# Second weight of both feed-forward stages as seven block products, with its input kept in DRAM

## The chip, the cores and the metric

One core of a Trainium2 chip. The metric is the time of the device in microseconds for one launch; the time before is the median of three runs. Matmuls work on float32r operands: every float32 operand is split into a high and a low part, and a product is formed from three matmuls (high x high, high x low, low x high), written `mm3` below.

## The reference

One layer of a streaming encoder for 1024 prompt tokens and 64 sample tokens (1088 columns in all), model width 1024, feed-forward width 2816:

```
h = LN1(alpha*x + 0.5*SwiGLU1(x))
z = h @ w_in; o_a = sparse attention; o_b = chunk-band attention
m = (sigmoid(g_a)*(o_a@w_branch_a) + sigmoid(g_b)*(o_b@w_branch_b)) @ w_out
h = LN2(alpha*h + m)
y = LN3(alpha*h + 0.5*SwiGLU2(h))
SwiGLU(x) = (silu(x@wi_left) * (x@wi_right)) @ wo
```

The two SwiGLU stages are what the change touches. Their first weight `wi` is 1024 x 5632, their second weight `wo` 2816 x 1024.

## The kernel before

Everything is kept transposed: features on the 128 partitions, tokens along the free dimension. `add_ffn7` (line 878) lays down one feed-forward stage as a list of steps; it is called once for each stage, with the bags `G1` and `G2` that hold the stage's tiles.

The 2816 inner features are 22 blocks `f` of 128. Blocks 0 and 1 are computed plainly (`plain`, line 1069). From block 2 on, the first weight is multiplied in Strassen-Winograd form (`product`, line 990): the 1024 input features are halved (2 x 4 parts), the 1088 tokens are halved (`HT` = 544 each), and the two weight columns of a block (left and right of the SwiGLU) are the other halves. Seven products P1, P2, P6, P5, P3, P7, P4 take the place of eight. Each is 2 token quarters (`SUB` = 272 columns) by 4 parts by 3 matmuls, 24 matmuls. Their right factors (tiles A11, A12, A22, S1, S2, S3, S4) are made once per stage: the A by splitting the input, the S by sums (`combos`, line 849; S3, in `third`, goes through the tile `G.t[0]`, named c, which `after` also uses for the copy of P1's bank and for the finished h). Their left factors are weight quarters and differences of them, made per block in `prepare` (line 910).

`after` (line 1024) takes the products from PSUM, applies silu and the product of both halves, and `h_parts` (line 1106) splits the finished h into high and low in a ring of two blocks in SBUF. P5 of a block goes on in the bank that ScalarE has just copied, and P6 goes on in P1's bank, so each waits for that copy (`wait(t[...])` in `product`).

The second weight is multiplied for two blocks at a time (`outputs`, line 1130): for each of 8 output parts `d` and 3 token blocks `b` of 384, 384 and 320 columns, 6 matmuls, then one VectorE addition from PSUM into the float32 tile `y`. This step follows P2 of the next even block; for blocks 0 and 1 it stands between P2 and P6 of block 2. Nine pairs go this way; the last four blocks (18 to 21) are multiplied in `last_outputs` (line 1139), part by part together with the layer norm. The last two blocks, 20 and 21, are computed side by side: P1 and P2 of both, then the other five of each.

Weights come from DRAM in quarters of 128 x 512 on the queue of SyncE (SP), into four to six raw buffers; four split buffers hold what TensorE reads. The order of the instructions is made while the program is built: `Plan` keeps a modelled clock of each engine, tasks have dependencies and priorities, and after every three matmuls (`tick`) the tasks whose modelled start has come are written out. Each engine runs its list in order, and a DMA on SP's list waits there for what it needs. For a task that several engines could take, `shared` and `adders` name VectorE and GpSimd; at the start of each stage (`st["solo"]`, until step `SOLO` = 7) VectorE alone takes them.

## Time and profile before

| | us |
|---|---|
| median of 3 runs | 2550.02 (2547.7 to 2554.39) |
| the profiled execution | 2550.51 |
| its span, first to last instruction | 2548.7 |
| granted TensorE clock, mean over the span | 0.988 |

The first feed-forward stage fills the span up to about 754 us, projections and attention the middle, the second stage begins near 1770 us. Names of engines in the profile: PE is TensorE, DVE VectorE, ACT ScalarE, POOL GpSimd, SP SyncE. Every instruction is recorded at line 119, a helper, so they are told apart by tiles: b is a PSUM bank, w_s a split weight, A and S right factors, h the ring, c the three tiles of `G.t`, y the float32 stream. Matmuls overlap, so a matmul's own duration says little; starts of following groups do.

### The profile page before, as it was taken

How to read it: one execution, taken by the hardware profiler on the slowest of the kernel's cores; microseconds unless marked ns; L12 is line 12 of the kernel's file. 1: busy time of each engine (PE TensorE's matmuls, PEld its weight loads, DVE VectorE, ACT ScalarE, POOL GpSimd, SP SyncE). 2: the span in 40 equal slices, each digit the busy share in tenths (PEclk: the TensorE clock that was granted, in tenths of full speed). 3: DMA queues.
4: the chain of work that ended last, by engine and by line, in shares of the span. 5: the costliest groups of instructions: out<-in, count | busy, mean ns of one | idle time of the engine just before them, and what ended most of it. 6: DMA issues, size and time to landing. Idle time of an engine off the chain costs nothing.

```text
span 2548.7 us, 44883 instructions
## 1 busy us (share of the span) xinstructions
PE 2482.5 (97%) x16906; PEld 2430.8 (95%) x16906; DVE 1794.8 (70%) x4447; ACT 1193.0 (47%) x2561; POOL 387.5 (15%) x515
## 2 busy tenths in 40 slices
PE   9999999999999999999999999999999999999996
PEld 9999999999998999999998999998999999999996
DVE  7666666666675889988676766748866666666667
ACT  5322222223344698677867776515532333222224
POOL 0000000000043322222243432304000000000004
PEclk9999999999998999999999999999999999999997
DMA  5122222111122322223221121643212121111112
GB/s 167 57 69 75 68 67 68 55 59 59 59 73 94 117 75 80 92 78 90 67 80 51 56 64 45 211 131 114 62 59 59 59 59 55 55 54 59 54 51 75
DMA packets 121866, 192.74 MB, mean 76 GB/s; under 512 B 14048, under 2 KB 74832, under 8 KB 121616
## 3 DMA queue, kind: packets, MB, share of 16 engines
q1 hardware_dynamic: 101536, 164.84, 21.2%
q10 hardware_dynamic: 19552, 22.81, 2.9%
q8 instruction: 133, 2.18, 0.4%
q0 software_dynamic: 560, 2.21, 0.2%
q14 instruction: 85, 0.70, 0.1%
HBM read 154.01 MB, written 36.07 MB: 75 GB/s over the span
## 4 chain that ended last, share of the span: by engine, by line
PE 79%; DVE 10%; ACT 6%; issue 2%; POOL 1%; DMA 1%; ACTq 0%; SPq 0%; DVEq 0%; POOLq 0%
PE b L119 79%; ACT w L119 2%; DVE w L119 1%; DVE y L119 1%; DVE w_s L119 1%; ACT scores L119 1%; DVE pt L119 1%; DVE scores L119 1%; DVE c L119 1%; ACT pt L119 1%; DVE k L119 0%; POOL lns L119 0%; DVE sc L119 0%; POOL w_s L119 0%; DVE mk L119 0%
## 5 line engine op out<-in xcount | busy, mean ns | idle before, releaser
L119 PE MATMUL b<-x,w_s 128*128 128x384 f32 (+1 forms) x3528 | 639.4, 332 | 5.1 <-ACT x L119 2.3
L119 PEld LDWEIGHTS b<-x,w_s 128*128 128x128 f32 x3528 | 586.9, 189 | 12.8 <-ACT x L119 2.9
L119 PE MATMUL b<-S,w_s 128*128 128x272 f32 x4032 | 514.3, 288 | 0.0
L119 PEld LDWEIGHTS b<-S,w_s 128*128 128x128 f32 x4032 | 508.6, 188 | 1.0 <-issue 0.6
L119 PE MATMUL b<-A,w_s 128*128 128x272 f32 (+2 forms) x3600 | 477.8, 292 | 3.0 <-ACT c L119 1.3
L119 ACT ACTIVATE w_s<-wr 128x512 fp32r<-128x512 f32 (+1 forms) x318 | 212.7, 670 | 571.4 <-PE b L119 395.1
L119 PEld LDWEIGHTS b<-A,w_s 128*128 128x128 f32 x3600 | 465.6, 190 | 7.5 <-ACT c L119 1.5
L119 PE MATMUL b<-h,w_s 128*128 128x384 f32 (+1 forms) x2736 | 463.8, 328 | 2.8 <-DVE y L119 2.8
L119 PEld LDWEIGHTS b<-h,w_s 128*128 128x128 f32 x2736 | 455.0, 188 | 5.1 <-DVE y L119 3.4
L119 DVE TENSOR_TENSOR w_s<-wr,w_s 128x512 fp32r<-128x512 f32 (+1 forms) x297 | 220.3, 742 | 166.0 <-ACT w_s L119 159.0
L119 DVE TENSOR_TENSOR y<-y,b 128x384 f32<-128x384 f32 (+1 forms) x480 | 251.0, 529 | 119.6 <-PE b L119 117.7
L119 POOL TENSOR_TENSOR w_s<-wr,w_s 128x256 fp32r<-128x256 f32 x196 | 151.8, 800 | 395.6 <-ACT w_s L119 177.7
L119 POOL TENSOR_TENSOR h<-c,h 128x272 fp32r<-128x272 f32 x20 | 15.5, 777 | 1240.5 <-DVE h L119 1239.1
L119 DVE TENSOR_TENSOR c<-c,b 128x272 f32<-128x272 f32 x240 | 103.7, 434 | 74.2 <-PE b L119 74.0
L119 ACT ACTIVATE c<-b 128x272 f32<-128x272 f32 (+1 forms) x262 | 102.0, 391 | 99.5 <-PE b L119 95.7
L119 DVE TENSOR_TENSOR pt<-b,pt 128x512 fp32r<-128x512 f32 (+4 forms) x184 | 96.3, 545 | 28.6 <-ACT pt L119 27.1
L119 ACT ACTIVATE c<-c 128x272 f32<-128x272 f32 x160 | 69.0, 432 | 93.3 <-DVE c L119 91.4
L119 PE MATMUL b<-pt,v 128*128 128x256 f32 (+3 forms) x672 | 103.6, 280 | 4.6 <-DVE pt L119 2.6
L119 PEld LDWEIGHTS b<-pt,v 128*128 128x128 f32 (+1 forms) x672 | 93.8, 188 | 13.5 <-DVE pt L119 5.1
L119 PE MATMUL b<-m,w_s 128*128 128x384 f32 (+1 forms) x576 | 101.5, 337 | 4.0 <-DVE w_s L119 3.8
L119 ACT ACTIVATE w<-w,mx 128x640 f32<-128x640 f32 (+5 forms) x144 | 100.5, 698 | 8.9 <-DVE mx L119 5.8
L119 PEld LDWEIGHTS b<-m,w_s 128*128 128x128 f32 x576 | 98.5, 194 | 5.7 <-DVE w_s L119 4.7
(262 smaller groups left out, 2963.8 us busy)
## 6 DMA issues: line engine op xcount, KB each, us to landing
wr<-in_wi_dram SPq DMA_DIRECT2D x166, 256.0 KB, 2.6
wr<-in_wz_dram SPq DMA_DIRECT2D x35, 512.0 KB, 3.6
wr<-in_wo_dram SPq DMA_DIRECT2D x47, 256.0 KB, 2.8
more<-in_wi_dram SPq DMA_DIRECT2D x38, 256.0 KB, 2.6
wr<-in_wout_dram SPq DMA_DIRECT2D x16, 512.0 KB, 3.8
q<-in_wi_dram SPq DMA_DIRECT2D x28, 256.0 KB, 2.6
g_d<-z ACTq DMA_DIRECT2D x32, 192.0 KB, 1.9
g<-g_d SPq DMA_DIRECT2D x32, 192.0 KB, 2.9
```

What stands on the lines that cost most here:

```text
L119: r = real(*args, **kw)
```

## The change

Of the 22 blocks, the first 18 (`KEPT_OUT`) are no longer multiplied with the second weight as they come. The finished h of each (float32, not split) is written to a DRAM array `ff_d` (`keep`). When the first weight is done, a second part multiplies them, nine pairs in Strassen-Winograd form: the two blocks of a pair are the halves of the inner dimension, the eight output parts are halved (4 and 4), and the tokens are halved. The seven kinds of products come one kind after the other, nine pairs each, and accumulate over the pairs in the eight PSUM banks; 63 products of 4 parts by 2 token quarters by 3 matmuls of 272 columns. After each kind `take_out` adds the banks to y.

The right factors come from h read back (36 tiles `G.a` of 128 x 544), with sums made in place and split into 5 factor buffers (`left`). The weight differences are made in the first part, at P1 of blocks 4 to 12 (`sums_of_weights`), and kept in DRAM (`tw_d`). The tiles of the second part take the memory of the first part's right factors (`to_second1`, `to_second2`). Blocks 18 and 19 are kept in the ring and multiplied as before: output parts 0 and 1 in `early`, between the two parts, the rest in `last_outputs`. Blocks 2 and 3 are computed side by side, as 20 and 21 are. The stream that prepares the bias tables in the first stage starts at block 4.

```diff
+KEPT_OUT = 18
...
+    ff_d = [dram.tile([KEPT_OUT * P, NT], F32, name=f"ff_d{i}") for i in range(2)]
+    tw_d = [dram.tile([P, 2 * KEPT_OUT * 512], F32, name=f"tw_d{i}") for i in range(2)]
...
-            second = f == NF - 1
+            second = f in SECONDS
...
+            def times(name, x, y, deps, cols, reads=()):
+                def go():
+                    nc.vector.scalar_tensor_tensor(x, x, 0.5, y, op0=OP.mult, op1=OP.mult)
+                    keep(f, x, cols)
+                t[name, s] = plan.task("dve", "f_m", go, deps, 1, None, reads)
...
+        def keep(f, x, cols):
+            if f < KEPT_OUT:
+                nc.sync.dma_start(ff[f * P:(f + 1) * P, cols], x)
+
+        def h_parts(o, x, cols, dep):
+            if o.f < KEPT_OUT:
+                return dep
+            h = o.h
...
-        def outputs(f0):
+        def early():
+
+            f0 = KEPT_OUT
             wait(*(F[f].t[x, s] for f in (f0, f0 + 1) for x in ("h1", "h2") for s in range(2)))
-            for i in OUTS[f0 == 0]:
-                u = get_unit(f"o{i}", f0)
-                for d in (2 * i, 2 * i + 1):
-                    for b in range(3):
-                        out_products([f0, f0 + 1], d, b, u.slot, (d % 2) * 2)
-                done_with(u)
+            wait(*G.sums_made)
+            roles.update(mm=[0, 1, 2, 3])
+            for t in range(4):
+                wait(*users.pop(t, ()))
+            G.to_second()
+            G.loads = [(n, j) for n in ("12", "11") for j in range(PAIRS)] + [(n, j) for j in range(PAIRS) for n in ("21", "22")]
+            load(0)
+            for i in range(len(G.fac)):
+                left(i)
+            u = get_unit("o0", f0)
+            for d in (0, 1):
+                for b in range(3):
+                    out_products([f0, f0 + 1], d, b, u.slot, (d % 2) * 2)
+                touched.update((d, half, s) for half in range(2) for s in range(2))
+            done_with(u)
+
+        def load(i):
+
+            while G.loads and 4 * PAIRS - len(G.loads) < 5 + 1.45 * i:
+                n, j = G.loads.pop(0)
+                back.add((n, j))
+                f, half = 2 * j + int(n[1]) - 1, int(n[0]) - 1
+                nc.sync.dma_start(G.a[n, j], ff[f * P:(f + 1) * P, half * HT:(half + 1) * HT])
+
+        def sums_of_weights(j):
+
+            r = G.stage[j % 2]
+            for i in range(4):
+                nc.sync.dma_start(r[i].rearrange("p (d c) -> p d c", d=4),
+                                  wog[:, i % 2 * 4:i % 2 * 4 + 4, (2 * j + i // 2) * P:(2 * j + i // 2 + 1) * P])
+            last = ()
+            for i, out, x, y in ((0, 0, 1, 0), (1, 1, 3, 1), (2, 3, 3, 0), (3, 2, 2, 3)):
+                def go(e, i=i, out=out, x=x, y=y):
+                    of(e).tensor_tensor(r[out], r[x], r[y], op=OP.subtract)
+                    nc.sync.dma_start(tw[:, (4 * j + i) * 512:(4 * j + i + 1) * 512], r[out])
+                last = [plan.task(shared(512), "w_x", go, last, 6, None, [r[x], r[y]])]
+            G.sums_made += last
+
+        def left(i):
+
+            x, j = SECOND[i // PAIRS], i % PAIRS
+            a11, a12, a21, a22 = (G.a[n, j] for n in ("11", "12", "21", "22"))
+            fac = G.fac[i % len(G.fac)]
+
+            def make(out, x, y, op, deps, reads=()):
+                return plan.task(shared(HT), "x_m", lambda e: of(e).tensor_tensor(out, x, y, op=op), deps, 2, None, reads)
+            y, deps = {"P2": a12, "P1": a11, "P6": a11, "P5": a21, "P3": a12, "P7": a11, "P4": a22}[x], []
+            if x == "P6":
+                t1 = sums_of[1, j] = make(a21, a21, a22, OP.add, [], [a21, a22])
+                deps = [make(a11, a21, a11, OP.subtract, [t1] + made["P1", j])]
+                sums_of[2, j] = deps[0]
+            elif x == "P5":
+                deps = [sums_of[1, j]]
+            elif x == "P3":
+                deps = [make(a12, a12, a11, OP.subtract, [sums_of[2, j]] + made["P2", j])]
+                sums_of[4, j] = deps[0]
+            elif x == "P7":
+                deps = [make(a11, a22, a11, OP.subtract, [sums_of[4, j]] + made["P6", j])]
+
+            def hi(e):
+                if e == "act":
+                    nc.scalar.activation(fac[:, 0], y, AF.Copy)
+                else:
+                    nc.vector.tensor_copy(fac[:, 0], y)
+
+            def lo(e):
+                of(e).tensor_tensor(fac[:, 1], y, fac[:, 0].bitcast(F32), op=OP.subtract)
+            assert {(n, j) for n in NEEDS[x]} <= back
+            t1 = plan.task((("act", 93 + 0.84 * HT), ("dve", WH * (69 + 0.52 * HT))), "x_h", hi, deps, 2, None, [y])
+            made[x, j] = [t1, plan.task(adders(HT), "x_l", lo, [t1], 2)]
+
+        def second(i):
+
+            x, j = SECOND[i // PAIRS], i % PAIRS
+            u = get_unit("x" + x, j)
+            wait(*made[x, j])
+            fac, first, final = G.fac[i % len(G.fac)], x in ("P2", "P1", "P7"), j == PAIRS - 1
+            for d in range(4):
+                c = slice(d * P, (d + 1) * P)
+                for s in range(2):
+                    if j == 0 and first:
+                        banks[d, s] = take_bank(2 * d + s)
+                    elif j == 0:
+                        wait(outs[d, s])
+                    p, v = banks[d, s][:, :SUB], fac[:, :, s * SUB:(s + 1) * SUB]
+                    nc.tensor.matmul(p, u.slot[:, 0, c], v[:, 0], start=first and j == 0, stop=False, skip_group_check=True)
+                    nc.tensor.matmul(p, u.slot[:, 0, c], v[:, 1], start=False, stop=False, skip_group_check=True)
+                    nc.tensor.matmul(p, u.slot[:, 1, c], v[:, 0], start=False, stop=final, skip_group_check=True)
+                    tick()
+                    if final:
+                        take_out(x, d, s, p)
+            done_with(u)
+            load(i + 1)
+            if i + len(G.fac) < len(SECOND) * PAIRS:
+                left(i + len(G.fac))
...
+        def take_out(x, d4, s, p):
+            half, d = {"P2": (0, 0), "P1": (0, 0), "P6": (1, 0), "P5": (1, 4), "P3": (0, 4), "P7": (1, 4), "P4": (1, 0)}[x]
+            d += d4
+            y = G.y[d][:, half * HT + s * SUB:half * HT + (s + 1) * SUB]
+            fresh = (d, half, s) not in touched
+            touched.add((d, half, s))
+            if fresh:
+                wait(*G.read[d])
+
+            def go():
+                if fresh:
+                    nc.vector.scalar_tensor_tensor(y, y, ALPHA, p, op0=OP.mult, op1=OP.add)
+                else:
+                    nc.vector.tensor_tensor(y, y, p, op=OP.add)
+            outs[d4, s] = outs[d, half, s, 0] = plan.task("dve", "f_y", go, (), 1, None, [p])
+            if x in ("P2", "P3", "P4"):
+                users[2 * d4 + s] = [outs[d4, s]]
...
+                    wait(*(outs[d, half, s, 0] for half in range(1 + (b > 0)) for s in range(2)))
+                    skip = 2 * (d < 2)
+                    out_products(fs[skip:], d, b, us[d].slot, skip)
...
-        for f in range(EIGHT, NF - 2):
+        def side_by_side(f):
+            return [(x, (f, f + 1)) for x in ("P1", "P2")] + [(x, (g,)) for g in (f, f + 1) for x in FACTOR if x > "P2"]
+        order += side_by_side(EIGHT)
+        for f in range(EIGHT + 2, NF - 2):
+            if f == EIGHT + 2:
+                order.append(("beside", (f,)))
+            if f == KEPT_OUT:
+                order.append(("ring", (f,)))
             for x in FACTOR:
-                if f == 3 and x == "P1" and gi == 0:
-                    order.append(("beside", (f,)))
                 order.append((x, (f,)))
-                if x == "P2" and f % 2 == 0:
-                    order.append(("out", (f - 2,)))
-        last_two = (NF - 2, NF - 1)
-        order += [(x, last_two) for x in ("P1", "P2")] + [(x, (f,)) for f in last_two for x in FACTOR if x > "P2"]
+                if x == "P1" and f - EIGHT - 2 < PAIRS:
+                    order.append(("sums", (f - EIGHT - 2,)))
+        order += side_by_side(NF - 2)
+        order += [("early", (KEPT_OUT,))] + [("second", (i,)) for i in range(len(SECOND) * PAIRS)]
...
+                elif x == "second":
+                    y, j = SECOND[f // PAIRS], f % PAIRS
+                    block = {"P2": (1, 0), "P1": (0, 0), "P3": (1, 1)}.get(y)
+                    if block:
+                        row, col = block
+                        want.append((("x" + y, j), lambda q: q.rearrange("p (d c) -> p d c", d=4),
+                                     wog[:, 4 * col:4 * col + 4, (2 * j + row) * P:(2 * j + row + 1) * P]))
+                    else:
+                        i = 4 * j + {"P5": 0, "P7": 1, "P6": 2, "P4": 3}[y]
+                        want.append((("x" + y, j), lambda q: q, tw[:, i * 512:(i + 1) * 512]))
+                    unit("x" + y, j)
+                    steps.append(lambda f=f: second(f))
...
+    SECONDS = (EIGHT + 1, NF - 1)
+    SECOND, PAIRS = ("P2", "P1", "P6", "P5", "P3", "P7", "P4"), KEPT_OUT // 2
+    NEEDS = dict(P2=("12",), P1=("11",), P6=("11", "21", "22"), P5=(), P3=(), P7=(), P4=())
...
+        G.a = {(x, j): p.tile([P, HT], F32, name=f"a{x}_{j}") for x in ("12", "11", "21", "22") for j in range(KEPT_OUT // 2)}
+        return [p.tile([P, 2, HT], F32R, name=f"fac{i}") for i in range(n)]
...
+    def to_second1():
+        close("x")
+        G1.fac = second_tiles(G1, pool(open_("x"), "back1", "right"), 5)
...
+    def to_second2():
+        close("s4")
+        close("s")
+        G2.fac = [G2.xc["A12"][:, k] for k in range(4)] + second_tiles(G2, pool(open_("s"), "back2"), 1)
```

## Rows read from the trace of the kernel before

**Rows 1.** Page, part 1: engine, busy us (share of the span), instructions.

```profile
PE 2482.5 (97%) x16906; PEld 2430.8 (95%) x16906; DVE 1794.8 (70%) x4447; ACT 1193.0 (47%) x2561; POOL 387.5 (15%) x515
```

**Rows 2.** Waits of TensorE, 90 to 600, then 1860 to 2510: us, times, longest.

```profile
PE b L119 <- DVE c L119: 0.2, 1, 0.2
...
PE b L119 <- DVE acc L119: 0.5, 1, 0.5
```

**Rows 3.** Timeline, TensorE, one output pair per stage: start us, us, what, [idle before].

```profile
602.39 23.98 PE L119 MATMUL b<-h,w_s 128*128 128x384 f32 x144
626.21 12.13 PE L119 MATMUL b<-S,w_s 128*128 128x272 f32 x96
638.18 9.16 PE L119 MATMUL b<-A,w_s 128*128 128x272 f32 x72
...
2363.05 24.10 PE L119 MATMUL b<-h,w_s 128*128 128x384 f32 x144
2386.99 12.19 PE L119 MATMUL b<-S,w_s 128*128 128x272 f32 x96
...
2399.03 9.18 PE L119 MATMUL b<-A,w_s 128*128 128x272 f32 x72
```

**Rows 4.** Timeline, TensorE, last output products of the first stage.

```profile
716.70 1.20 PE L119 MATMUL b<-h,w_e 128*128 128x384 f32 x6
...
747.83 1.04 PE L119 MATMUL b<-A,w_i 128*128 128x320 f32 x6
```

**Rows 5.** Timeline, TensorE, output product of blocks 0 and 1, both stages.

```profile
63.90 3.12 PE L119 MATMUL b<-h,w_s 128*128 128x384 f32 x18
68.72 21.12 PE L119 MATMUL b<-h,w_s 128*128 128x384 f32 x126 [1.70 <-DVE y L119]
...
1833.39 4.21 PE L119 MATMUL b<-h,w_s 128*128 128x384 f32 x24
1838.68 20.17 PE L119 MATMUL b<-h,w_s 128*128 128x384 f32 x120 [1.08 <-DVE y L119]
```

**Rows 6.** Timeline, VectorE, first and last of the S3 sums, both stages.

```profile
61.98 0.73 DVE L119 TENSOR_TENSOR c<-y 128x544 f32<-128x544 f32 x1
...
71.64 0.72 DVE L119 TENSOR_TENSOR S<-c,S 128x544 fp32r<-128x544 f32 x1
...
1833.17 0.72 DVE L119 TENSOR_TENSOR c<-y 128x544 f32<-128x544 f32 x1
...
1849.37 0.72 DVE L119 TENSOR_TENSOR S<-c,S 128x544 fp32r<-128x544 f32 x1
```

**Rows 7.** Timeline, ScalarE, the copy behind them in the first stage.

```profile
72.39 0.69 ACT L119 ACTIVATE c<-b 128x272 f32<-128x272 f32 x2 [0.90 <-DVE S L119]
```

**Rows 8.** Groups by shape: xcount | busy us, mean ns | idle before.

```profile
L119 DVE TENSOR_TENSOR w_s<-wr,w_s 128x512 fp32r<-128x512 f32 x285 | 203.0, 713 | 165.4 <-ACT w_s L119 158.4 <-DMA g<-g_d 0.4
...
L119 DVE TENSOR_TENSOR c<-c,b 128x272 f32<-128x272 f32 x240 | 103.7, 434 | 74.2 <-PE b L119 74.0
...
L119 DVE TENSOR_TENSOR S<-c,S 128x544 fp32r<-128x544 f32 x32 | 22.8, 721 | 6.4 <-ACT S L119 5.8
L119 ACT ACTIVATE S<-c 128x544 fp32r<-128x544 f32 x32 | 20.6, 656 | 37.3 <-DVE c L119 37.3
```

**Rows 9.** DMA issues: tiles, queue, xcount, KB each, us to landing.

```profile
wr<-in_wo_dram SPq DMA_DIRECT2D x47, 256.0 KB, 2.8
...
o_d<-o SPq DMA_DIRECT2D x32, 128.0 KB, 1.7
```

**Rows 10.** Timeline, TensorE, a wait early in the second stage.

```profile
1788.65 1.28 PE L119 MATMUL b<-ones,lns 128*128 128x1 f32 x6 [2.70 <-DVE lns L119]
```

**Rows 11.** Windows: us, busy of PE PEld DVE ACT POOL, PEclk, DMA share, GB/s.

```profile
1788.20:1794.80 6.60, 6.15 (x28) 6.15 (x29) 2.25 (x6) 2.69 (x5) 0.00 (x0) 0.50 0.16 47
...
662.00:704.00 42.00, 42.00 (x338) 42.00 (x338) 28.95 (x59) 15.14 (x32) 1.55 (x2) 1.00 0.22 66
1593.00:1657.00 64.00, 61.16 (x357) 58.96 (x356) 49.10 (x89) 38.03 (x64) 23.45 (x23) 1.00 0.66 211
```

More of the change, by code (lines that the diff above doesn't have):

```diff
@@ L883, in add_ffn7 @@
         free, src, want, units, by, users = list(G.free), {}, [], [], {}, {}
+        ff, tw = ff_d[gi // 2], tw_d[gi // 2]
+        sums_of, made, outs, banks, touched, back = {}, {}, {}, {}, set(), set()
         at, low, F, ACC, Y = Bag(), {}, {}, {}, {}
@@ L1054, in after @@
             elif kind == "P3":
-                times("m1", c, p, [t["s1", s]], [p])
+                times("m1", c, p, [t["s1", s]], one, [p])
                 users[base + s] = [t["m1", s]]
-                t["h1", s] = h_parts(h, c, one, t["m1", s])
+                t["h1", s] = h_parts(o, c, one, t["m1", s])
                 G.user[0, s] = [t["h1", s]]
@@ L1064, in after @@
                 silu("s2", c21, t["c21", s])
-                times("m2", c21, c22, [t["s2", s], t["c22", s]])
-                t["h2", s] = h_parts(h, c21, two, t["m2", s])
+                times("m2", c21, c22, [t["s2", s], t["c22", s]], two)
+                t["h2", s] = h_parts(o, c21, two, t["m2", s])
                 G.user[1, s], G.user[2, s] = [t["h2", s]], [t["m2", s]]
@@ L1123, in out_products @@
             y = Y[d, b]
-            if fs[0] == 0:
+            if (d, 0, 0) not in touched:
                 wait(*G.read[d])
@@ L1262, in tile_trunk, with stage_tiles, ring_tile, second_tiles @@
     factors(G1, sorted(set(FACTOR.values()) - {"A11"}), x1)
-    G1.ring = rp.tile([P, 2, 2, NT], F32R, name="h")
     G1.t = [rp.tile([P, 2, SUB], F32, name=f"c{i}") for i in range(3)]
-    flip, btab = rp.tile([P, P], F32, name="flip"), rp.tile([P, 2, HEADS], F32, name="btab")
     raw_tiles(G1)
     G1.q += [rp.tile([P, 512], F32, name=f"q{i}") for i in range(2)]
-    G1.free, G1.kept = range(5), 5
+    def stage_tiles(G, name, side):
+        p = pool(open_(name), name, side)
+        G.stage = [[p.tile([P, 512], F32, name=f"st{x}{i}") for i in range(4)] for x in range(2)]
+        return p
+    def ring_tile(G, name, side):
+        close(name)
+        G.ring = pool(open_(name), name, side).tile([P, 2, 2, NT], F32R, name="h")
+    def second_tiles(G, p, n):
+        G.a = {(x, j): p.tile([P, HT], F32, name=f"a{x}_{j}") for x in ("12", "11", "21", "22") for j in range(KEPT_OUT // 2)}
+        return [p.tile([P, 2, HT], F32R, name=f"fac{i}") for i in range(n)]
+    p1 = stage_tiles(G1, "top1", None)
+    flip, btab = p1.tile([P, P], F32, name="flip"), p1.tile([P, 2, HEADS], F32, name="btab")
+    def make_ring1():
+        finish_streams()
+        ring_tile(G1, "top1", None)
+    G1.make_ring = make_ring1
+    def to_second1():
+        close("x")
+        G1.fac = second_tiles(G1, pool(open_("x"), "back1", "right"), 5)
+    G1.to_second = to_second1
+    G1.free, G1.one = range(6), rp.tile([P, 512], F32, name="one")
     def halves_of(w, home):
@@ L1286, in bias_tables @@
     def bias_tables():
-        one = G1.q[G1.kept]
+        one = G1.one
         row = one[:HEADS, :384]
@@ L1326, in bias_tables, with start_bias @@
                 yield
-    def start_bias(after):
-        def go():
-            yield from bias_tables()
-            for _ in range(8):
-                yield
-            roles.update(mm=[4, 5, 6, 7])
-            after()
-        beside(go(), 0.3)
+    def start_bias():
+        beside(bias_tables(), 0.3)
     def load_x(half, row, k):
```

51 lines of the change are left out of this document (28 added, 23 removed).

## The prediction

> **What bounds the kernel now.** I read the busy table of the page first: TensorE works for 2482.5 of 2548.7 us, VectorE for 1794.8 [rows 1]. Busy time alone could hide stalls, so the second view is what TensorE waited for: between 90 and 600 us one wait of 0.2 us, between 1860 and 2510 us one of 0.5 us [rows 2]. In both feed-forward stages, then, the time is the number of matmuls by their spacing. What the change takes from that sum arrives in full, and what counts against it is only time in which TensorE has to wait.
>
> **What it removes and adds on TensorE.** The second weight's product of one pair of blocks is 144 matmuls of 384 and 320 columns. In the first stage one such pair starts at 602.39 and what follows starts at 626.21: 23.82 us. In the second stage 2363.05 to 2386.99: 23.94 us [rows 3]. The new form has per pair seven products of 24 matmuls of 272 columns, 168 in all. The trace has that shape in the first weight's products: 96 from 626.21 to 638.18, 124.7 ns each, and 96 from 2386.99 to 2399.03, 125.4 ns each [rows 3]. So a pair costs 20.95 and 21.07 us instead: 2.87 us less nine times, and again 2.87 us nine times, together 51.7 us. The 36 matmuls for blocks 18 and 19 on output parts 0 and 1 come earlier, and their six evictions are one addition more per tile; the count is the same.
>
> Does the spacing of 272 columns hold in the new loop, which changes its accumulator every 3 matmuls instead of every 12? The output products change theirs after 6 (pairs) or 12 (last four blocks), and six of 384 show 1.20 us, six of 320 show 1.04 us: 0.16 us for 6 x 64 columns, 0.42 ns a column, what 2.4 GHz gives [rows 4]. I take 124.7 and 125.4 ns as they stand; 5 ns a matmul more would cost 2 x 1512 x 5 ns = 15 us.
>
> On the other side stands the Trainium skill, "TensorE: Matmul & The Clock Gate", section "Back-to-back issue gap": in a real stream it gives about 81 ns a matmul at 128 columns and about 131 ns at 512. Interpolated (an estimate), a pair would be 16.1 us before and 16.8 us after, and the change would lose about 12 us instead of gaining 52. The trace speaks against it: 512 is not reached and 272 columns already take 124.7 ns.
>
> **Start of the seven products (block 2).** Now the output product of blocks 0 and 1 stands between P2 and P6 of block 2. TensorE waited 1.70 us in it in the first stage and 1.08 us in the second, since the additions into y wait for the factor sums to have read y [rows 5]. These 2.8 us go. But those 24 us are also the cover for VectorE's last factor sums, S3. They begin when the plain blocks are done with the tile c: 61.98 us, and the last of four ends at 72.36; second stage 1833.17 and 1850.09 [rows 6]. P1's copy out of its bank into that same c comes right behind, at 72.39 [rows 7], and P6 of block 2 accumulates in the bank that it copies. Today P6 comes only when the output product ends, near 89.8, so nobody notices. Afterwards only P1 and P2 of block 3 stand between (48 matmuls, 6.0 us): P6 is due 6.0 us after the point where the output product starts today, at 69.9 and 1839.4 [rows 5].
>
> How late is c then? The S3 chain is serial through one tile: sum 0.72, copy on ScalarE 0.66, rest on VectorE 0.72 [rows 8], 2.1 us by itself, 2.4 to 2.6 us with weight splits in between, 10 us for four. Evictions and the split of h no longer interleave, but c first has to be written to DRAM: a 136 KB write, between the 128 KB write that lands 1.7 us after issue [rows 9] and a little more. So its start stays at about 62.5 and 1833, its end is about 72.5 to 74 and 1843 to 1844.5, and with the copy TensorE waits 3 to 4.5 and 4 to 5.5 us. I take 3.5 and 4.3, 7.8 together; the bounds are 0 (VectorE free sooner) and 12.
>
> A gap like that can cost the clock: after a 2.70 us wait that ended at 1788.65 [rows 10], with a shorter one before it, the stretch 1788.2 to 1794.8 shows a granted clock of 0.50, the lower level of 1.2 GHz [rows 11]. Half speed over 3.3 to 6.6 us loses 1.7 to 3.3 us each time. I add 1.7 us per stage: 3.4, bounds 0 and 6.6.
>
> Block 3, begun side by side with block 2, reuses the tile of c21 after only one product instead of three; its read by the DRAM write (1.7 us) takes the place of the split of h, a copy and a rest half as wide as those of rows 8, about as long. I take 0.5 us per stage: 1.0, bounds 0 and 4.
>
> **Main loop, blocks 4 to 17.** Without output products between, each block's 21 us carries on VectorE: its own work, 28.95 us in 42 us where two blocks run back to back, 69% [rows 11]; plus, in nine of them, four differences of second-weight blocks of 0.7 us, 13%; minus the splits of h. At most 82%, ScalarE at 36%: hidden under the products. Without that cover 2.8 us a block would show, 50 us in all, first as waits of TensorE on c. The DRAM writes of h stand in SP's queue behind the weight loads; their tiles are wanted again 2.5 products (7 us) later, against about 2 us of write. Nothing.
>
> **Into the second part.** After P4 of block 21 come the 36 early output matmuls: 6.0 us of cover. The first left factor needs its load, one copy (0.66) and one rest (0.72). In the first stage the loads overwrite factors used long before, so they start early; in the second they overwrite A22, which P4 reads last, and start only now: 2.8 us as for a weight quarter [rows 9], up to 4 with five in a row, plus 1.4 and two hand-overs, 5 to 6 us. I take 1.0 us and 1.5 us, the wait for the banks of the last early evictions included: 2.5, bounds 0 and 8.
>
> **Inside the second part.** It is 63 products of 3.0 us, 189 us. VectorE has 63 splits of weights at 0.713, 63 rests of factors at 0.721, 36 sums at 0.721 and 56 evictions at 0.434 [rows 8]: 45 + 45 + 26 + 24 = 140 us, 74%, if GpSimd takes none. ScalarE: 2 x 63 copies at no more than 0.656 are 83 us. The tightest stretch is P6: two sums per product, 2.9 of 3.0 us, but it is prepared five products ahead. At the end of each of the seven kinds eight evictions come at once; the next product wants the last of these banks 2.6 us after its last matmul, and the pile then is 8 x 0.434 - 7 x 0.374 = 0.9 us plus one other operation of 0.7. That fits; I take 0.2 us at each of 12 changes, 2.4 in all; bounds 0 and 24 (2 us each).
>
> Loads: the back-loaded h is asked for at 1.45 tiles per product until 36 are in, 1.45 x 279 KB + 262 KB in 3.0 us: 222 GB/s over the first third. The trace moved 211 GB/s over 64 us with its engines 66% busy [rows 11], which would allow 320. Hidden, with less to spare than anywhere else.
>
> **End.** The last output products no longer wait for blocks 20 and 21, but there was no wait to win [rows 2]; four weight slots come from memory that the second part holds to its end, and are wanted 6 us later. I take 0.5 us per stage: 1.0.
>
> **Sum.** 51.7 + 2.8 = 54.5 us off; 7.8 + 3.4 + 1.0 + 2.5 + 2.4 + 1.0 = 18.1 us on; net 36.4. The profiled execution took 2550.51 us (span 2548.7 and 1.8 around it), 0.5 over the median of 2550.02, so the sum can be set against either: 2514 us. The attention between the stages is planned from the same state but not the same clock; its order may shift, a few us either way, and I count none.
>
> **Rivals.**
> 1. Every cover holds: S3 is in time, no bank is waited for. 54.5 us off: 2496. For it: VectorE loses 216 evictions a stage. Against it: S3's chain is latency, not load. Chance 0.17.
> 2. VectorE becomes the bound in the second part: its 74% come in bunches, P6 at 97% and behind it the evictions of P1. With 2 us at each of the 12 changes, 22 more: 2536. Chance 0.13.
> 3. Slower: the back-loads are not delivered. 31 tiles and 21 weight quarters, 14.1 MB, should pass in 63 us. If DRAM reads and SP's issues give less than about 170 GB/s, that third takes 83 us and eats the net 18 us a stage; at 140 GB/s it takes 101 us, 38 us over each time: 2590. From 170 GB/s down it decides. For it: one queue, and 512-byte pieces in three of the seven weight views. Against it: 211 GB/s in the row. Chance 0.05.
> 4. Slower: the number of matmuls counts, not their columns. If each cost the same, 23.82 us / 144 = 165 ns, 24 more per pair and 18 pairs would be 71 us: 2622; with half of the spacing fixed, (71 - 52) / 2 = 10 us: 2560. This is the direction of the Trainium skill's rule in "Back-to-back issue gap". The 0.42 ns a column refute it here. Chance 0.02.
> 5. The gain is spent in places not named, above all in an attention that is planned worse: within 8 us of before. Chance 0.03.
>
> My forecast has 0.60. Its own range is 2502 to 2528; with the cases beside it, 2497 to 2537 leaves out about two in ten. 0.3% is 7.7 us, about what a measurement of this kernel tells from no change: faster 0.90, same 0.04, slower 0.06.
>
> **What would show it.** In the changed kernel's profile: 24 matmuls of 272 columns in 3.0 us throughout the second part, in each stage some 189 us of them; a wait of TensorE of 3 to 5 us on ScalarE's copy or VectorE ahead of block 2's P6, near 70 and near 1820; a granted clock of 0.50 shortly behind it; a wait under 2 us ahead of the second part; DMA near 220 GB/s in its first third. The prediction is wrong if the spacing of 272 columns is above 130 ns in the second part, or if its products wait on VectorE or DMA by more than 10 us a stage.

## The result, and the profile after

The changed kernel takes 2535.1 us (median of 4 runs, 2532.6 to 2537.4); the kernel before, beside it, 2551.1 (2547.7 to 2554.4). The ratio is 0.9937, with an interval of 0.992 to 0.9954: faster, but by 16 us instead of the 36 that were forecast. The profiled spans say the same: 2548.7 before, 2532.5 after. First the page of the changed kernel: engine, busy us (share of the span), instructions; then the line of its DMA packets and three lines of its DMA issues (tiles, queue, count, KB each, median us from issue to landing). In these, a is h read back, st a block of the second weight loaded for a difference, wr a weight quarter.

```profile
PE 2438.6 (96%) x17338; PEld 2382.9 (94%) x17338; DVE 1797.7 (71%) x4263; ACT 1231.5 (49%) x2611; POOL 477.1 (19%) x561
...
DMA packets 221205, 285.42 MB, mean 113 GB/s; under 512 B 20704, under 2 KB 146512, under 8 KB 220944
...
a<-ff_d SPq DMA_DIRECT2D x72, 272.0 KB, 3.7
st<-in_wo_dram SPq DMA_DIRECT2D x72, 256.0 KB, 5.3
...
wr<-in_wo_dram SPq DMA_DIRECT2D x38, 256.0 KB, 2.9
```

Against [rows 1], TensorE lost 43.9 us of busy time but only 16.2 us of span. What left the sum of matmuls came partly back as waiting. That is the line to look for whenever a change shortens the work of the bounding engine: busy time and span should fall by the same amount, and here they don't.

The arithmetic of the matmuls held. In the timeline of TensorE (start us, us, what, [idle before]) four products of the new second part start at 2276.50 and what follows at 2288.56: 12.06 us, 125.6 ns a matmul (A in these rows is a factor buffer of the second part, which in the second stage lies in the memory of A12); the first weight's products of the same stage had 125.4 [rows 3].

```profile
2276.50 12.22 PE L120 MATMUL b<-A,w_s 128*128 128x272 f32 x96
2288.56 3.18 PE L120 MATMUL b<-fac,w_s 128*128 128x272 f32 x24
```

What did not hold are the covers. The waits of TensorE (us in total, times, longest) in the main loop of the first stage, 110 to 420 us, where the prediction counted nothing and the kernel before had next to nothing [rows 2]:

```profile
PE b L120 <- ACT c L120: 6.4, 5, 2.1
```

and the larger waits in its timeline: before P6 of block 2 (75.63 and 1842.02), into the second part (512.61 and 2259.86), at the change from P1 to P6 in the second part (570.95 and 2317.26) and at the end (2504.26).

```profile
75.63 14.35 PE L120 MATMUL b<-S,w_s 128*128 128x272 f32 x96 [4.22 <-ACT c L120]
...
512.61 55.96 PE L120 MATMUL b<-fac,w_s 128*128 128x272 f32 x432 [2.05 <-DVE y L120]
...
570.95 9.26 PE L120 MATMUL b<-fac,w_s 128*128 128x272 f32 x60 [2.37 <-DVE y L120]
...
1842.02 13.54 PE L120 MATMUL b<-S,w_s 128*128 128x272 f32 x96 [6.25 <-ACT c L120]
...
2259.86 13.79 PE L120 MATMUL b<-A,w_s 128*128 128x272 f32 x96 [1.99 <-DVE y L120]
...
2317.26 2.98 PE L120 MATMUL b<-A,w_s 128*128 128x272 f32 x22 [1.42 <-DVE y L120]
...
2504.26 1.20 PE L120 MATMUL b<-ones,rest 128*80 128x1 f32 x8 [6.66 <-DVE rest L120]
```

In the kernel before, the wait at the end is half as long:

```profile
2519.81 1.20 PE L119 MATMUL b<-ones,rest 128*80 128x1 f32 x8 [3.33 <-DVE rest L119]
```

Behind several of them the matmuls run slower. A row of 96 without a stop takes 12.22 us, 12.06 by the starts and 0.16 for the end of its last matmul; the 96 at 75.63 take 14.35, and the 60 at 570.95 take 9.26, where 7.70 would do. The windows (us; busy of PE, PEld, DVE, ACT, POOL; PEclk; DMA share; GB/s) show a granted clock of 0.50 and 0.60 there, the level of 1.2 GHz and a mix of it with 2.4 GHz. Behind the stop of 1.42 us at 2317.26 the clock stays at 1.00:

```profile
75.60:80.00 4.40, 4.37 (x19) 4.37 (x20) 0.79 (x2) 1.45 (x4) 0.00 (x0) 0.50 0.26 89
...
570.90:575.00 4.10, 4.05 (x21) 4.08 (x22) 4.10 (x10) 0.66 (x1) 2.07 (x2) 0.60 0.66 208
2317.00:2320.50 3.50, 3.24 (x26) 3.27 (x27) 3.50 (x9) 0.75 (x2) 3.42 (x3) 1.00 0.80 266
```

Where in the span the time went is seen from two points that every one of these kernels has: the first matmul of the product of x behind the first feed-forward stage (753.99 before, 752.13 after), and the wait for the norm early in the second stage (1788.65 before, 1784.46 after, [rows 10]). The first stage gained 1.9 us, what lies between 2.3 (the change does not touch it), the second stage 12.0.

Why the main loop waits is read from VectorE and then ScalarE. On VectorE, a difference of two second-weight blocks waits 4.31 us for its load while it is at the head of the engine's order, and an addition of c, which needs nothing from it, comes only behind (TensorE had finished its product by 181.49):

```profile
180.15 0.44 DVE L120 TENSOR_TENSOR c<-c,b 128x272 f32<-128x272 f32 x1 [0.23 <-PE b L120]
184.90 0.69 DVE L120 TENSOR_TENSOR st<-st,st 128x512 f32<-128x512 f32 x1 [4.31 <-DMA st<-in_wo_dram]
185.51 0.43 DVE L120 TENSOR_TENSOR c<-c,b 128x272 f32<-128x272 f32 x1
```

ScalarE's next operation on c stands for it, and TensorE for the bank that ScalarE copies out behind that:

```profile
185.97 0.43 ACT L120 ACTIVATE c<-c 128x272 f32<-128x272 f32 x1 [3.77 <-DVE c L120]
186.31 0.38 ACT L120 ACTIVATE c<-b 128x272 f32<-128x272 f32 x1
```

```profile
186.74 3.51 PE L120 MATMUL b<-S,w_s 128*128 128x272 f32 x26 [2.13 <-ACT c L120]
```

VectorE waits 34 times in this way, 46.4 us in all: 25.9 in the first stage's main loop, and 20.5 in the second's, at most 3.0 at a time. There TensorE's cover is enough: between 1870 and 2180 us it doesn't wait once. What makes the first stage tighter (the stream of the bias tables runs only there) was not tested. The order in which VectorE works was written by the planner, whose model lets a load of 256 KB on an idle queue end 1.4 + 0.73 + 0.3 = 2.4 us after its issue (the constants of `count`); these land after 5.3.

### The profile page after: what moved, and what is told of

It reads as the page before. It is cut to its first block, busy times and chain, and to the rows that moved or that the text cites. A ratio compares the mean times of both kernels' runs of the same rounds, so it can differ in the third digit from the quotient of the medians.

```text
span 2532.5 us, 46846 instructions
## 1 busy us (share of the span) xinstructions
PE 2438.6 (96%) x17338; PEld 2382.9 (94%) x17338; DVE 1797.7 (71%) x4263; ACT 1231.5 (49%) x2611; POOL 477.1 (19%) x561
## 4 chain that ended last, share of the span: by engine, by line
PE 71%; DVE 11%; ACT 9%; issue 3%; DMA 3%; POOL 1%; ACTq 1%; SPq 0%; DVEq 0%; POOLq 0%
PE b L120 71%; ACT w L120 3%; ACT scores L120 2%; DVE w_s L120 2%; DVE y L120 1%; DVE w L120 1%; DVE k L120 1%; ACT pt L120 1%; DVE c L120 1%; DMA st<-in_wo_dram 1%; DVE pt L120 1%; ACT z L120 1%; DMA a<-ff_d 1%; DMA ff_d<-c 1%; ACTq L120 1%
## 5 line engine op out<-in xcount | busy, mean ns | idle before, releaser
L120 PE MATMUL b<-A,w_s 128*128 128x272 f32 (+1 forms) x4824 | 633.9, 291 | 7.8 <-DVE y L120 3.4
L120 PEld LDWEIGHTS b<-A,w_s 128*128 128x128 f32 x4824 | 620.9, 190 | 12.1 <-ACT A L120 2.6
L120 PE MATMUL b<-S,w_s 128*128 128x272 f32 x4032 | 520.4, 289 | 18.2 <-ACT c L120 18.2
L120 ACT ACTIVATE w_s<-wr 128x512 fp32r<-128x512 f32 (+1 forms) x270 | 181.1, 671 | 368.5 <-PE b L120 223.1
L120 DVE TENSOR_TENSOR w_s<-wr,w_s 128x512 fp32r<-128x512 f32 (+1 forms) x323 | 247.4, 768 | 151.6 <-ACT w_s L120 142.3
L120 PE MATMUL b<-fac,w_s 128*128 128x272 f32 x1800 | 231.4, 290 | 4.4 <-DVE y L120 4.4
L120 PEld LDWEIGHTS b<-fac,w_s 128*128 128x128 f32 x1800 | 229.8, 190 | 4.9 <-issue 2.6
L120 POOL TENSOR_TENSOR h<-c,h 128x272 fp32r<-128x272 f32 x2 | 1.5, 773 | 902.7 <-DVE h L120 902.7
L120 ACT ACTIVATE fac<-a 128x544 fp32r<-128x544 f32 x75 | 49.4, 658 | 142.0 <-PE b L120 121.4
L120 ACT ACTIVATE w<-w,sm 128x640 f32<-128x640 f32 (+5 forms) x144 | 97.7, 697 | 9.7 <-DVE sm L120 4.6
```

The source lines that it names most:

```text
L120: r = real(*args, **kw)
```

## The experiments

Twelve kernels were run, each beside the kernel before. Their names are those that the expectations use. "Ratio" is against the kernel before; the changed kernel has 0.9937.

**e1_late: the planner told that these loads land later.** Theory: the late waits are an order written for earlier landings. Rival: VectorE has too much to do, or is held up by GpSimd.

```
             e, end = "dma", self.dma + 300
+            if outs[0].tensor.name.startswith(("st", "a1", "a2")):
+                end += 4000
```

> The changed kernel with one edit: in the planner's own model a load into the stage tiles (st), the difference tiles of the second weight (a11, a12, a21, a22) ends 4 us later, so that what reads them is written later in VectorE's and GpSimd's order. Theory A (late loads stand at the head of in-order engines: the planner believed in earlier landings, the difference of st waits up to 4.31 us on VectorE, and the copies of the bias table and of the sums behind it are late): the five main-loop waits of 6.4 us of the first stage fall below 2 us, the waits into the second part (2.05 and 1.99 us) and before P6 in it (2.37 and 1.42 us) shrink as well; 5 to 12 us less than the changed kernel, 2523 to 2530 us. Theory B (VectorE simply has more to do, and is held by GpSimd's work beside it): an order that is written later helps nothing, waits within 1 us of the old ones, 2533 to 2540 us.

Measured: 2518.4 us, ratio 0.9879 (0.9864 to 0.9894). Of TensorE's waits between 90 and 600 us only this is left (it was 6.9 us on c and 4.4 on y):

```profile
PE b L120 <- ACT c L120: 1.5, 2, 0.8
```

The loads land no sooner (median 5.1 us), VectorE is busy as long as before (1791.7 us for 1797.7), but its waits for them are gone:

```profile
DVE st L120 <- DMA st<-in_wo_dram: 0.3, 1, 0.3
```

and the second part starts and goes on without a stop:

```profile
503.95 8.26 PE L120 MATMUL b<-fac,w_s 128*128 128x272 f32 x61
...
554.73 17.49 PE L120 MATMUL b<-fac,w_s 128*128 128x272 f32 x138
```

Theory A, and by more than its range. Nothing was taken out: VectorE, ScalarE and GpSimd have 7435 instructions together in both kernels. What changed is their order, and with it the engine of a few (GpSimd has 550 for 561). About as much came back as the whole change had gained; of the 15.7 us between the profiled spans 13.9 lie in the first stage and 2.0 in the second.

**e6_st: the same for the loads of the second weight alone.**

> As the run e1_late, but with the 4 us more for the loads into the stage tiles st alone; the reloads into a11 to a22 stand in the planner's model as in the changed kernel. Theory A (two separate costs: the late st loads make the main-loop waits of the first stage, the late reloads those into the second part and before P6 in it): the main-loop waits are gone as in e1_late (6.4 us less), the waits of 2.4 and 2.3 us into the second part and of 2.7 and 1.7 us before P6 stay; 2526 to 2530 us. Theory B (the late st loads displace all that follows): all of these are gone, as in e1_late; 2517 to 2521 us.

Measured: 2528.3 us, ratio 0.9919 (0.9904 to 0.9933). The main loop of the first stage waits 0.3 us instead of 6.4, as in e1_late. The second part still begins with a wait of 1.27 us at 503.68 in the first stage, and before P6 of the second part TensorE's matmul starts lie 3.8 us apart in each stage, where they were 2.7 and 1.7 in the changed kernel. Theory A: two separate late loads, each with its own stops.

**e12_late2 and e13_late8: 2 us and 8 us instead of 4** (in the setting of e10_banks, below).

> As e10_banks, with 2 us more in the planner's model for the loads instead of 4. Theory A (the loads land 2 to 4 us later than modelled, so half the correction leaves part of the stops): 2 to 8 us more than e10_banks, 2504 to 2510 us. Theory B (any shift of the order does it): within 2 us of e10_banks.

> As e10_banks, with 8 us more instead of 4. Theory A (at 4 us the order already fits the landings; more only writes the sums later than needed): 0 to 8 us more than e10_banks. Theory B (the landings have a tail beyond 4 us that still costs): 2 to 5 us less than e10_banks.

Measured: 2511.0 us, ratio 0.9853 (0.9838 to 0.9867) with 2 us, and 2516.7 us, ratio 0.9876 (0.9856 to 0.9896) with 8 us, against 0.982 with 4. With 2 us VectorE still waits, less, and the stop before P6 of the second part is back:

```profile
DVE st L120 <- DMA st<-in_wo_dram: 20.3, 23, 2.4
```

```profile
553.58 6.66 PE L120 MATMUL b<-fac,w_s 128*128 128x272 f32 x39 [2.50 <-DVE y L120]
```

With 8 us half of the differences (37 of 72) go to GpSimd, which waits for the loads up to 16.3 us at a time, and TensorE has a stop of 2.57 us at 248.08. Theory A of both, and each costs more than its range said (2504 to 2510 us, and at most 8 us over e10_banks, where 14 were measured). A due time can be wrong on both sides.

**e2_s3: the last factor sums without the tile c.** The four sums S3 of block 2 take the first two sums' tiles in turn.

```
-            m3 = make(s3, a11, a21, OP.subtract, G.used(0), [])
-            use(0, [factor(G, "S3", k, s3, [m3])])
+            i, x = 1 + k % 2, (s1, s2)[k % 2]
+            m3 = make(x, a11, a21, OP.subtract, G.used(i), [])
+            use(i, [factor(G, "S3", k, x, [m3])])
```

> The changed kernel with one edit: the third sums of block 2 (S3, four pairs) are put into the buffers of the first two sums in turn instead of into the buffer c that the product before last reads, so that they need not wait until c's last copy went to DRAM. Theory A (block 2 waits before P6 because S3 waits for c to be free): the waits of 4.22 and 6.25 us before P6 go to under 1 us each, and the 12 matmuls after them are back at 12.1 us from 14.35 and 13.54; 10 to 14 us less, 2521 to 2525 us. Theory B (the wait is VectorE's load of sums and weight differences in block 2, whatever buffer they go to): the sums start no more than 1 us earlier, the two waits stay above 6 us in sum; 2532 to 2537 us.

Measured: 2525.0 us, ratio 0.9906 (0.9891 to 0.9922). In the changed kernel the first S3 sum starts at 63.28, after 2.01 us of wait for the write of c to DRAM, and the last ends at 75.15; P1's copy into c follows at 75.18. Here the waits before P6 are 0.29 and 1.15 us, and what follows runs near full speed:

```profile
73.72 6.51 PE L120 MATMUL b<-S,w_s 128*128 128x272 f32 x50 [0.29 <-ACT c L120]
...
1833.51 9.28 PE L120 MATMUL b<-S,w_s 128*128 128x272 f32 x72 [1.15 <-ACT c L120]
```

The mechanism is theory A's. The time lies at the edge of its range; by the ratios, which take out the kernel before, the gain is 7.9 us and smaller than the 10 to 14. By the profile the first stage is 8.8 us shorter; the second is only 0.8 us shorter: of what block 2 won there, 2.2 us went in a gap of 3.9 us between matmul starts before P6 of the second part that was 1.7 us in the changed kernel, and about as much in slower matmuls behind it. The late reloads were still there to take it.

**e8_late_s3: both.**

> Both edits of e1_late and e2_s3 together. Theory A (two independent mechanisms, each with its own stops): the gains add up, 14.8 + 7.9 to 10 us less than the changed kernel, 2508 to 2512 us; gaps before P6 of block 2 under 1.5 us, main loop and second part as in e1_late. Theory B (both shorten the same queue on VectorE): about the better of the two alone, 2516 to 2519 us.

Measured: 2504.4 us, ratio 0.9825 (0.981 to 0.984). Against the changed kernel that is 0.0112; e1_late has 0.0058 and e2_s3 0.0031, together 0.0089, and their intervals allow the difference. Theory A, with more gain than its range. By the profile the second stage is 8.5 us shorter than in the changed kernel, where e2_s3 alone had 0.8: once the reloads no longer stop the second part, what block 2 gains is kept to the end.

**e3_banks: six banks for the early output products instead of four.**

```
-            roles.update(mm=[0, 1, 2, 3])
-            for t in range(4):
+            roles.update(mm=[0, 1, 2, 3, 4, 5])
+            turn["mm"] = 0
+            for t in range(6):
```

> The changed kernel with one edit: the first output products of each feed-forward stage go over six PSUM banks instead of four, so the second user of a bank comes two products later. Theory A (TensorE stands into the second part because an eviction on VectorE is behind a sum that waits for its reload): the waits of 2.05 and 1.99 us there go below 1 us each, and the half-clock stretch behind them with them; 3 to 7 us less, 2528 to 2532 us. Theory B (the stop moves to the next product that needs what the late reload gives): a wait of the same size stands some products later; 2533 to 2537 us.

Measured: 2530.3 us, ratio 0.9925 (0.991 to 0.994), which lies within the interval of the changed kernel; by time alone no difference is shown. The waits into the second part are gone; the first stage, where the early products now run on into the second part:

```profile
502.31 6.15 PE L120 MATMUL b<-h,w_s 128*128 128x384 f32 x36
508.30 7.99 PE L120 MATMUL b<-fac,w_s 128*128 128x272 f32 x61
```

So that stop is an eviction, queued on VectorE behind the rest of a factor whose reload was late (a rest of 1.45 us at 510.55, the evictions at 511.92, P2 at 512.61). The gaps before P6 of the second part stay, at 2.3 and 2.4 us. By the profile the first stage is 7.6 us shorter and the second no shorter, while the attention between is 2.6 us longer.

**e10_banks: e8_late_s3 with the six banks.**

> As e8_late_s3, and besides the six banks of e3_banks for the early products. Theory A (the last 0.4 and 1.0 us into the second part are still an eviction): 1 to 2 us less than e8_late_s3. Theory B (with the reloads rightly placed the banks no longer matter): within 1 us of it.

Measured: 2502.3 us (2498.8 to 2505.0), ratio 0.982 (0.9803 to 0.9836), not to be told from e8_late_s3, so neither theory is decided. It has the lowest median of the study. Of TensorE's waits after 1850 us this one is left:

```profile
PE b L120 <- DVE rest L120: 6.6, 1, 6.6
```

and block 2 of the first stage goes straight through where the changed kernel stood 4.22 us (in the second stage 1.23 of 6.25 us are left):

```profile
70.19 12.24 PE L120 MATMUL b<-S,w_s 128*128 128x272 f32 x96
82.26 3.31 PE L120 MATMUL b<-A,w_s 128*128 128x272 f32 x24
```

**e4_dve: the sums of the second part on VectorE alone.**

```
-                return plan.task(shared(HT), "x_m", lambda e: ...
+                return plan.task(shared(HT)[:1], "x_m", lambda e: ...
```

> The changed kernel with one edit: the sums of the second part's inputs (x_m, which go to VectorE or GpSimd by the planner's choice) all go to VectorE. Theory A (while GpSimd adds beside it, an operation of VectorE takes 1.4 to 1.9 us instead of 0.4 to 0.7): VectorE's operations before P6 of the second part return to 0.4 to 0.8 us, the evictions start earlier, and the waits of 2.37 and 1.42 us fall below 1 us; 3 to 6 us less, 2529 to 2532 us. Theory B (the reloads are what is late, and one engine with all the sums is late by more): both waits grow by 1 to 3 us; 2536 to 2542 us.

Measured: 2525.0 us, ratio 0.9905 (0.9889 to 0.9922), more than expected; in the profile the first stage is 7.0 us shorter, the second no shorter, and 3.6 us belong to the attention between, which the edit does not touch. The stop before P6 is gone in both stages. First the changed kernel, VectorE, then GpSimd in the same stretch:

```profile
550.48 0.71 DVE L120 TENSOR_TENSOR fac<-a,fac 128x544 fp32r<-128x544 f32 x1
...
556.43 1.53 DVE L120 CAST w_s<-wr 128x512 fp32r<-128x512 f32 x1
558.07 1.66 DVE L120 TENSOR_TENSOR w_s<-wr,w_s 128x512 fp32r<-128x512 f32 x1
559.65 1.88 DVE L120 TENSOR_TENSOR fac<-a,fac 128x544 fp32r<-128x544 f32 x1
...
570.38 2.86 DVE L120 TENSOR_TENSOR y<-y,b 128x272 f32<-128x272 f32 x8
```

```profile
547.14 2.86 POOL L120 TENSOR_TENSOR a<-a,a 128x544 f32<-128x544 f32 x2 [6.34 <-DMA a<-ff_d]
554.08 10.17 POOL L120 TENSOR_TENSOR a<-a,a 128x544 f32<-128x544 f32 x6 [4.08 <-DMA a<-ff_d]
```

Six sums on GpSimd stand from 554.08 to 564.25, 1.7 us each, and in that time the operations of VectorE that take 0.42, 0.69 and 0.71 us elsewhere take 1.5 to 1.9. The eight evictions behind them begin at 570.38, 2 us after P1's last matmul (which starts at 568.29). In e4_dve the sums take 0.74 us on VectorE, and its other operations keep their times:

```profile
558.16 0.72 DVE L120 TENSOR_TENSOR fac<-a,fac 128x544 fp32r<-128x544 f32 x1
558.79 1.48 DVE L120 TENSOR_TENSOR a<-a,a 128x544 f32<-128x544 f32 x2
560.24 0.69 DVE L120 TENSOR_TENSOR w_s<-wr,w_s 128x512 fp32r<-128x512 f32 x1
```

The Trainium skill, "SBUF — State Buffer", section "SBUF: two separate sides", has VectorE and GpSimd share a pair of ports; an instruction that needs it (on VectorE one with both inputs in SBUF, or in a mode that uses both ports) holds it to its end, and the other engine waits. The trace agrees in this stretch: 0.71 becomes 1.88 us, by less than one GpSimd sum, while the evictions, which have one input in PSUM, took 0.36 us each by their spacing beside the GpSimd sums that follow at 568.39.

**e7_all: e10_banks with that edit.**

> The four edits of e1_late, e2_s3, e3_banks and e4_dve together (that is e10_banks with the x_m sums on VectorE alone). Theory A (late loads and GpSimd's sums beside VectorE are two ways to the same stop before P6 of the second part; once the order fits the loads, the sums on GpSimd cost nothing): within 3 us of e10_banks, 2499 to 2506 us. Theory B (the slow VectorE operations beside GpSimd cost TensorE elsewhere too): 3 to 8 us less than e10_banks, 2494 to 2499 us.

Measured: 2505.1 us, ratio 0.9826 (0.9811 to 0.9841): nothing more. Theory A. The stop before P6 takes both, reloads later than the order expects and GpSimd's sums beside VectorE: e1_late takes away the first, e4_dve the second, and either alone ends it. With the order right the sums on GpSimd cost nothing that these runs can tell.

**e9_noearly and e14_half: the early output products put back, all and half of them.** Both touch the products of blocks 18 and 19; the first starts from e8_late_s3, the second from e10_banks.

```
-            u = get_unit("o0", f0)
-            for d in (0, 1):                    # e14_half: for d in (0,):
-                for b in range(3):
-                    out_products([f0, f0 + 1], d, b, u.slot, (d % 2) * 2)
...
-                    skip = 2 * (d < 2)
+                    skip = 0                    # e14_half: skip = 2 * (d < 1)
```

> As e8_late_s3, and besides the output products of the first two 128-columns of blocks 18 and 19 are no longer done early, before the second part, but at the end of the stage as in the kernel before. Theory A (the last products are the cover of the norm's work on VectorE, GpSimd and ScalarE, and the early products took 6 to 8 us of it away): TensorE's last wait falls from 6.7 to about 3.3 us, and the wait into the second part grows by at most 2 us as its inputs then load later than wanted; 1 to 4 us less than e8_late_s3. Theory B (the early products are what covers the turn into the second part): that wait grows by 4 us or more in each stage; 4 to 10 us more than e8_late_s3.

> As e10_banks, with only half of the early output products (of the first of the two output blocks): the other half goes back to the stage's end. Theory A (both the turn into the second part and the norm at the end need some 3 us of cover, and half of the products is enough for each): TensorE's last wait falls from 6.6 to about 5 us and no wait into the second part over 1 us; 1 to 2 us less than e10_banks. Theory B (the turn needs all of them): the wait into the second part comes back with 1.5 us or more in each stage; 1 to 4 us more than e10_banks.

Measured for e9_noearly: 2504.7 us, ratio 0.9831 (0.9816 to 0.9845), the same as e8_late_s3, which neither theory forecast; each is half right. The wait at the end is back at the 3.33 us of the kernel before, as theory A said, but the turn into the second part costs 3.4 to 3.7 us in each stage, more than A allowed and less than B's 4:

```profile
494.27 0.51 PE L120 MATMUL b<-fac,w_s 128*128 128x272 f32 x1 [3.67 <-ACT fac L120]
...
2234.54 0.39 PE L120 MATMUL b<-A,w_s 128*128 128x272 f32 x1 [3.35 <-ACT A L120]
...
2481.21 1.20 PE L120 MATMUL b<-ones,rest 128*80 128x1 f32 x8 [3.33 <-DVE rest L120]
```

Measured for e14_half: 2518.1 us, ratio 0.988 (0.9866 to 0.9895), 16 us more than e10_banks, outside both theories. The end waits 3.86 us, and the turn 1.17 and 0.82 us in the first stage. By the profile 9 of the 20 us that its span is longer than that of e10_banks lie in the attention between the stages, 7 in the first stage and 4 in the second. Most of the 9 us shows in the granted clock: in e14_half it is 0.94 over 1060 to 1090 us (behind a wait of 3.97 us at 1072.51, which is 0.92 in e10_banks), 0.83 over 1355 to 1375 and 0.93 over 1630 to 1655; in e10_banks it is 1.00 in the same work, 1053 to 1083, 1345 to 1365 and 1620 to 1645. That makes 0.06 x 30 + 0.17 x 20 + 0.07 x 25, some 7 us, an estimate that holds if TensorE was the limit there. Why TensorE stood longer in front of these stretches was not tested.

## Why the prediction fell short, step by step

The right side of the sum held: 51.7 us by the spacing of 272 columns (125.6 ns measured for 124.7 and 125.4 taken) and the 2.8 us of waits on the outputs of blocks 0 and 1. In e10_banks, where few stops are left, the first stage is 24.3 us shorter than before and the second 24.3, for 27.2 each without any stop. The rule of the Trainium skill that the prediction weighed against it ("TensorE: Matmul & The Clock Gate", section "Back-to-back issue gap") would have had the new form lose; the trace does not agree, with 125.6 ns at 272 columns. The other side, which was 18.1 us:

| step | predicted | measured in the changed kernel | what it was |
|---|---|---|---|
| P6 of block 2 waits for c | 7.8 | 4.22 + 6.25 = 10.5 | as described; e2_s3 takes it away |
| clock behind it | 3.4 | 2.1 + 1.3 = 3.4 | as described |
| block 3 | 1.0 | 0.53 + 0.87 = 1.4 | as described |
| main loop | 0 | 6.4 | late loads of st at the head of VectorE; e1_late, e6_st |
| into the second part | 2.5 | 4.0 and 3.1 of clock | eviction behind a late reload; e1_late, e3_banks |
| changes of kind | 2.4 | 3.8 and 1.6 of clock | GpSimd's sums beside VectorE behind late reloads; e1_late, e4_dve |
| end | 1.0 | 3.3 | the early products were the norm's cover; e9_noearly |

The clock's figures are worked out as above: the time of a row less 125.6 ns for each of its matmuls and 0.16 us for the last one's end (12.22 for the 96 at 75.63 and 1842.02). The sum is 37.5 us; 54.5 less that is 17.0 for a span that fell by 16.2. That it closes so well is in part luck. Between the stages 2.3 us were gained that no row of the table names; the first stage came out some 4.5 us worse than its rows (1.4 us of it in the first 10 us of the span) and the second some 1.5 better.

1. **The main loop, ending in "Nothing.", failed.** It compared busy shares, "At most 82%", and found room. The share was never the limit: VectorE is busy 62% in 110 to 200 us of the changed kernel and still waits. What the step left out is that an engine works in a fixed order and that the four differences per pair begin with a load. Where the change adds a wait, the question is what stands behind it in the queue; the step named the DMA queue's order (the writes of h behind the weight loads), not VectorE's. It gave the new loads no landing time at all: weight quarters of the same 256 KB land in 2.8 us [rows 9], the new loads in 5.3.
2. **Into the second part and changes of kind were sized as if no eviction stood behind a reload.** Their bounds, 0 to 8 and 0 to 24, held the 7.1 and 5.4, but at two to three times the 2.5 and 2.4. The step sized the factor by a load of up to 4 us, then put the evictions on an undisturbed VectorE. They stood behind the factor in its order.
3. **VectorE's 74% in the second part** was worked out for the case that GpSimd takes none, and counted GpSimd's help as a relief. Where the sums bunched it was the opposite: an operation of 0.71 us took 1.88. Rival 2, VectorE as the bound with 2536, has the right time and the wrong reason: only one of six changes per stage shows a wait over 1 us, and e1_late removes it with the same load on VectorE.
4. **The end.** "there was no wait to win" was read from the waits between 1860 and 2510 us [rows 2], which stop just short of the 3.33 us at 2519.81. Taking 6 us of products away from there doubled that wait; the prediction counted the 36 early matmuls at nothing because their number stays the same. What counted was their place, and they are worth as much at the turn as at the end: e9_noearly has the time of e8_late_s3.
5. **Block 2** was found with its mechanism, tile and consequence in the clock. Its size was off by 2.7 us: the four S3 sums take 11.9 us in each stage for the 10 taken, with weight differences of block 2 between the links of the chain on VectorE, and the second stage waits 6.25 for 4.3.

Neither sign by which the prediction wanted to be called wrong came up: the spacing is under 130 ns, and the second part's products wait 4.4 and 3.4 us a stage, under 10. No sign watched the main loop, where the first step failed.

That 1 and 2 are one cause, the order written from a model of the loads, is shown: e1_late changes only the planner's landing times, and 0.9937 becomes 0.9879. Rival 3, loads that can't be delivered, is out: the second part of e1_late runs without a stop at 219 GB/s (505 to 560 us). With the order and the buffer mended the forecast's 2514 is passed, at 2502; rival 1, all covers holding, had said 2496.

What stays open: why the st loads take 5.3 us. Pieces of 512 bytes are not the reason: the weight quarters of P1, P2 and P3 of the second part have the same view of the same tensor, and the wr among them land after 3.0 us (12 loads between 515 and 700 us). That the st come four at a time beside the other traffic of the main loop is left, and was not tested. Open too are the attention's own shifts of up to 9 us between kernels that don't touch it (in e14_half mostly a lower clock); they set a floor to what a few us of time can show here.

## What to carry to other kernels

Hiding by share is not hiding in order. For each operation that a change adds to an in-order engine, ask whether it starts with a load, when that load lands as measured under the new traffic, and which operation behind it the bounding engine waits for. And where a planner writes the order, a change that brings a new kind of load needs that load's landing in the planner's model: here 4 us in one line were worth about as much as the whole change. Work that is moved early out of a stage's end takes its cover along: look there for the wait that it used to hide.

## What the runs showed of the hardware that was not expected

- Loads of the same tensor, the same 256 KB and the same 512-byte pieces land after 5.3 us (st, four at a time) and 3.0 us (wr in the second part, 515 to 700 us), in one execution.
- Beside GpSimd's sums, VectorE's copies went from 0.41 to 1.53 us and its subtractions from 0.71 to 1.88; GpSimd's sums themselves went from 1.37 us (one alone at 575.11) to 1.7. Additions that read PSUM kept 0.36 us.
- A stop of 2.37 us was followed by a granted clock of 0.60 over 4.1 us; one of 1.42 us at the same place of the other stage, with the clock at 1.00 behind it, cost only itself. The length of the stop alone does not tell: 2.05 us at 512.61 brought a clock of 0.72 over 512 to 516 us, while 2.13 us at 186.74 left it at 1.00 (110 to 200 us).
